# Row sums of squares of a differential-attention head: from one-column float32 products to ScalarE squares on transposed tiles

## The chip, the cores and the metric

One core of one Trainium2 chip runs the whole layer. The metric is the device time of one launch in microseconds (us); less is better. The engines are named as in the profile: PE is the matrix engine (PEld its weight loads), DVE the vector engine, ACT the scalar engine (activations), POOL the general engine, SP the queue that issues most transfers. Each engine works through its own instructions in the order in which the program gives them, and an instruction that needs another engine's result waits at the head of its queue.

## The reference, cut to what matters

The layer has a token mixer (differential attention with four heads and sparse attention with eight heads that read the same input) and a feed-forward part. The change touches the end of a differential head only:

```python
def rms_norm(x, g):
    xf = x.astype(jnp.float32)
    y = xf * lax.rsqrt(jnp.mean(xf * xf, axis=-1, keepdims=True) + NORM_EPS)
    return (y * g.astype(jnp.float32)).astype(x.dtype)
...
    o_diff = diff_attention(dq, dk, dv, lam)
    o_diff = (rms_norm(o_diff, diff_subln) * (1.0 - lam_init)).reshape(B, S, DIFF_WIDTH)
```

For each of the 512 tokens and each of the four heads, the head's output has 128 values. The mean of their squares is needed, its inverse root scales the 128 values, and each of the 128 positions also has a gain of its own, `diff_subln * (1 - lam_init)`.

## The kernel before, in words

The kernel is written for a sequence of 512 tokens, four blocks of 128. In the attention part a differential head is called `D0` to `D3`, a sparse head `N0` to `N7`. The order of all work is written out by hand in a string called `PLAN`: each word is a step, and the steps are issued from first to last. So the place of a step in `PLAN` decides its place in the queue of every engine that it uses, relative to all other steps on that engine.

A step's name is the head, then the operation. The digits behind a colon choose the buffers that the step takes. For steps in which PE opens a new result tile, that digit is one of the eight PSUM banks: `N1S02:6` opens bank 6. A bank may be opened again only when everyone who reads its former content is done.

The operations that matter here:

- `S..` scores on PE, `Q..` the causal mask added on PE, `X..` the row maximum on DVE, `E..` the exponential on ACT with its row sum (an ACTIVATE, and behind it an instruction that reads the accumulator). `X` and `E` read the bank of `S`. `D1S00:6` puts the scores of two token blocks into bank 6, and `D1E01` and `D1E00` read them.
- `T..` PE transposes the probabilities into a bank; `H..` ACT copies them out rounded (line 983), `L..` DVE takes the rest (line 986); `V..` products with the values on PE (line 1034 for `D`, 1156 for `N`).
- `SC`, `CX`, `PH`, `TC`, `HC` belong to the compressed branch of a sparse head, `KS1` and `KF1` to the compressed values (lines 870, 883, 886). `M0` to `M3` are early products of the output projection (line 1227), which are long runs on PE alone.

A differential head's output stands transposed: the 128 value positions on the partitions, the 512 tokens along the row, in one bank called `av`. The end of the head is, in steps: `SQ` (ACT squares the bank into an SBUF tile, line 1039), `O3` (ACT copies the bank into an SBUF tile times the gain per partition, line 1043), `MS` (PE multiplies each 128x128 block of squares with a column of ones, so that the sums over the partitions come out with tokens on the partitions, four columns; line 1048), `N1` (DVE adds the epsilon; line 1052), `N2` and `N3` (ACT, logarithm and exponential), `N4` (POOL, one Newton step), `RB` (PE spreads the four columns back over the partitions by transposes, line 1064), `ML` (DVE multiplies, line 1082), `OH` and `OL` (the result split into two parts).

Around the four `MS` steps the plan before runs, cut to what stands next to them:

```
... D1E01:3 N2SC:0 D1X00:7 v1d0 N0H02:11 N0L02 N0M10 D1R D0MS:3 N0H00 N0L00 N2CX:11 KF1 D1E00:1 D1Q01 N0T10:7 N1S02:6 D0N1 N0H10:00 ...
... N5S1:0 ... N5Q01 D1MS:2 N5Q1 N5X12:0 N3H10:00 N3L10 N5E00:0 N5E12:3 N5X01:2 N4g1 N3T11:6 ...
```

Of the kernel before, what the change touches and what calls it, by code (L numbers as in the profile page):

```python
# [27 lines left out]
DIFF_HEADS = 4  # L28
# [84 lines left out]
N7S0:3 D3S11:7 N5H00 G1:1 N4O2:0 N5TC:4 D3Q11 N7Q0 N5L00 D3X12:0 N6S11:5 N5HC:1 N7X10:6 N6S02:6 N5V00:2 D3E12:3 D3R
# [171 lines left out]
def hybrid_block_kernel(  # L285
# [6 lines left out]
    act, dve, pool, pe = nc.scalar, nc.vector, nc.gpsimd, nc.tensor  # L292
# [6 lines left out]
    turn = [None]  # L299
# [702 lines left out]
    def diff_head(h, qd, kd, dv):  # L1002
        pp, hs = [{}, {}], {}
# [24 lines left out]
        def avs(u):  # L1028
            for j in JS[u]:
                if j == 0:  # L1030
                    hs["av"] = ps("av")
                for n, (vi, t) in enumerate(((0, 0), (1, 0), (0, 1))):
                    v0 = vi * 256 + (h % 2) * P
                    pe.matmul(hs["av"][:, j * P:], dv[j][:, v0:v0 + P], blocks(hs["pt"][t], j),  # L1034
                              start=(j == 0 and n == 0), stop=(j == NT - 1 and n == 2))

        def square():
            hs["sq"] = tslot("sq", tag="o")
            act.activation(hs["sq"], hs["av"], AF.Square)

        def weigh():
            hs["o32"] = tslot("o32", tag="o")
            act.activation(hs["o32"], hs["av"], AF.Copy, scale=gsub)

        def sums():
            hs["ms"] = ps("ms")
            for i in range(NT):
                pe.matmul(hs["ms"][:, i:i + 1], hs["sq"][:, i * P:(i + 1) * P], ones, start=True, stop=True)
# [17 lines left out]
        def out_high():  # L1066
# [9 lines left out]
        ops.update(  # L1076
            SQ=square, O3=weigh, MS=sums,
            N1=norm_in,
            N2=lambda: act.activation(hs["r"][1], hs["r"][0], AF.Ln),
            N3=lambda: act.activation(hs["r"][1], hs["r"][1], AF.Exp, scale=-0.5),  # L1080
            N4=newton, RB=spread,
            ML=lambda: dve.tensor_tensor(hs["sq"], hs["o32"], hs["rb"], OP.mult),
            OH=out_high,
# [243 lines left out]
    rr, pre, sq, rt, rv = ([None] * NT for _ in range(5))  # L1327
# [724 lines left out]
```

## Time and profile before

| what | value |
|---|---|
| time, median of 3 runs | 613.69 us (613.07 to 614.32) |
| the profiled execution's own time | 614.05 us |
| its span in the profile | 612.2 us |
| PE busy | 603.4 us, 99% of the span |
| DVE busy | 545.4 us, 89% |
| ACT busy | 373.7 us, 61% |
| POOL busy | 101.9 us, 17% |
| granted PE clock | 0.996 |

How to read it: the span is what the profile covers, and 614.05 minus 612.2, about 1.9 us, lies around it. The busy time of PE includes matrix products whose ends are modelled from a pipeline, so that a duration is longer than the distance to the next start; for the price of an instruction in a stream the distance between starts is the better number. ACT shows the same overlap: an ACTIVATE's duration is about 0.1 us longer than the distance to the next one. The timeline prints start and duration in us, engine, line, operation, output and inputs, and merges neighbours of one kind into one row with their count; a bracket at the end tells of idle time before it and who ended it. The windows view gives busy us of each engine in a stretch. The attention part with the four heads' ends runs from about 139 to 247 us of the span.

### The profile page before, as it was taken

Reading aid. Unit: us, or ns where it says so; the run is one execution under the profiler, and the core shown is the slowest. Engines: PE = TensorE matmul, PEld = TensorE weight load, DVE = VectorE, ACT = ScalarE, POOL = GpSimd, SP = SyncE. Lnnn points to the kernel's source line nnn. Section 1 sums busy time; section 2 is a strip of 40 time slices with the busy share of each in tenths; the row PEclk is TensorE's granted clock in tenths of the full one; section 3 lists DMA queues with packets and bytes.
Section 4 is the critical chain, followed back from the end, with each engine's and each line's share of the span. In section 5 each row is a group of like instructions: output and inputs, shape, how many; then the busy total and the mean of one; then the engine's idle time right before and its main releaser. Section 6 shows DMA issues by size and latency. Waiting matters only on the chain.

```text
span 612.2 us, 11013 instructions
## 1 busy us (share of the span) xinstructions
PE 603.4 (99%) x4066; PEld 548.5 (90%) x4066; DVE 545.4 (89%) x967; ACT 373.7 (61%) x784; POOL 101.9 (17%) x154
## 2 busy tenths in 40 slices
PE   9999999999999999999999999999999999999995
PEld 6888888899999989889999999999999988888884
DVE  5898888998899884899999998899999899999977
ACT  6445375467998886568585555555553666577522
POOL 0030000307868789100000000000000000000001
PEclk9999999999999999999999999999999999999998
DMA  8667786755342301654143444344342554576413
GB/s 260 204 221 276 243 308 229 247 210 187 105 122 90 101 35 39 203 201 177 38 171 105 138 138 138 105 139 172 124 138 84 173 172 164 186 247 229 137 40 133
DMA packets 38487, 98.42 MB, mean 161 GB/s; under 512 B 4257, under 2 KB 12065, under 8 KB 37537
## 3 DMA queue, kind: packets, MB, share of 16 engines
q1 hardware_dynamic: 38000, 97.45, 47.2%
q8 instruction: 32, 0.52, 0.4%
q10 hardware_dynamic: 432, 0.27, 0.1%
q14 instruction: 23, 0.18, 0.1%
HBM read 82.10 MB, written 15.60 MB: 160 GB/s over the span
## 4 chain that ended last, share of the span: by engine, by line
PE 91%; DVE 6%; DMA 1%; ACT 1%; issue 1%; DVEq 0%
PE yz L1494 26%; PE acc L1568 14%; PE fm L609 9%; PE fm L590 6%; PE mix L1241 5%; PE x L1494 4%; PE tr L973 4%; PE v L725 4%; PE avn L1156 3%; PE g L725 2%; PE sc L942 2%; PE sc L943 2%; PE mixp L1227 2%; PE cmp L824 1%; PE av L1034 1%; PE acc L1717 1%
## 5 line engine op out<-in xcount | busy, mean ns | idle before, releaser
L1774 POOL TENSOR_TENSOR uf<-c,gain 128x512 f32<-128x512 f32 x1 | 1.3, 1283 | 353.4 <-DVE c L1739 353.4
L956 ACT ACTIVATE p<-sc,nm 128x256 f32<-128x256 f32 (+3 forms) x96 | 50.5, 531 | 13.0 <-DVE nm L952 12.4
L952 DVE TENSOR_REDUCE nm<-sc 128x1 f32<-128x384 f32 (+3 forms) x96 | 43.0, 482 | 5.5 <-PE sc L948 3.4
L1494 PE MATMUL yz<-rope,wbh 128*128 128x256 f32 x352 | 47.2, 276 | 0.0
L1125 POOL TENSOR_TENSOR p<-p,l 128x256 f32<-128x256 f32 (+3 forms) x64 | 45.3, 732 | 0.9
L1494 PEld LDWEIGHTS yz<-rope,wbh 128*128 128x128 f32 x352 | 43.3, 188 | 0.0
L986 DVE TENSOR_TENSOR ptl<-tr,pth 128x384 fp32r<-128x384 f32 (+1 forms) x60 | 34.3, 591 | 8.8 <-ACT pth L983 8.8
L983 ACT ACTIVATE pth<-tr 128x384 fp32r<-128x384 f32 (+1 forms) x60 | 30.2, 528 | 6.9 <-PE tr L973 6.7
L1471 ACT ACTIVATE weh<-e 128x1024 fp32r<-128x1024 f32 x22 | 23.3, 1058 | 16.0 <-DVE e L1453 12.5
L1479 DVE TENSOR_TENSOR wel<-e,weh 128x1024 fp32r<-128x1024 f32 x22 | 26.8, 1220 | 3.4 <-ACT weh L1471 2.9
L1471 ACT ACTIVATE wbh<-wraw 128x1024 fp32r<-128x1024 f32 x22 | 23.3, 1059 | 10.3 <-DVE wraw L1458 6.4
L973 PE MATMUL tr<-ident,p 128*128 128x128 f32 x200 | 27.7, 273 | 0.0
L1479 DVE TENSOR_TENSOR wbl<-wraw,wbh 128x1024 fp32r<-128x1024 f32 x22 | 26.9, 1221 | 0.9 <-ACT wbh L1471 0.9
L1471 ACT ACTIVATE whi<-wraw 128x1024 fp32r<-128x1024 f32 x22 | 23.1, 1055 | 7.3 <-DMA wraw<-in_wg 7.1
L1617 ACT ACTIVATE whi<-wraw 128x1024 fp32r<-128x1024 f32 x20 | 21.0, 1056 | 10.7 <-PE acc L1568 6.5
L1494 PE MATMUL yz<-rope,wbl 128*128 128x256 f32 x176 | 27.2, 276 | 0.0
L1479 DVE TENSOR_TENSOR wlo<-wraw,whi 128x1024 fp32r<-128x1024 f32 x22 | 26.8, 1219 | 0.0
L1623 DVE TENSOR_TENSOR wlo<-wraw,whi 128x1024 fp32r<-128x1024 f32 x20 | 24.2, 1222 | 2.0 <-ACT whi L1617 2.0
L1494 PEld LDWEIGHTS yz<-rope,wbl 128*128 128x128 f32 x176 | 23.3, 188 | 0.0
L1524 ACT ACTIVATE us<-yz 128x512 f32<-128x512 f32 x22 | 13.0, 592 | 16.9 <-PE yz L1494 16.7
L973 PEld LDWEIGHTS tr<-ident,p 128*128 128x128 f32 x200 | 22.4, 141 | 0.7
L942 PE MATMUL sc<-kst,qst 128*128 128x384 f32 (+3 forms) x64 | 22.9, 366 | 0.0
(385 smaller groups left out, 1996.6 us busy)
## 6 DMA issues: line engine op xcount, KB each, us to landing
wraw<-in_wg SPq DMA_DIRECT2D x24, 512.0 KB, 3.7
wraw<-in_wu SPq DMA_DIRECT2D x22, 512.0 KB, 3.3
wraw<-in_wd SPq DMA_DIRECT2D x22, 512.0 KB, 3.7
qk<-rope SPq DMA_DIRECT2D x7, 1024.0 KB, 5.2
kst<-qk SPq DMA_DIRECT2D x24, 256.0 KB, 4.4
wraw<-in_wf SPq DMA_DIRECT2D x10, 512.0 KB, 4.7
wraw<-in_wo SPq DMA_DIRECT2D x8, 512.0 KB, 4.3
qst<-qk SPq DMA_DIRECT2D x16, 256.0 KB, 2.7
```

The source lines that it names most:

```text
L590: pe.matmul(st["fm", m][:, s], blk[k][w][:, m * P:(m + 1) * P], xx[k][:, s], start=first, stop=True, skip_group_check=True)
L609: pe.matmul(st["fm", m], fms[m][w][:, k * P:(k + 1) * P], xx[k], start=(c == 0 and k == 0), stop=(c == 2 and k == NK - 1))
L725: pe.matmul(pts[i], xx[k][:, i * P:(i + 1) * P], ws[c][wi][:, off:off + n], start=(m == 0), stop=(m == 3 * NK - 1))
L942: pe.matmul(sv[i], lhs, kk[:, 0, :w], start=(n == 0), stop=False, skip_group_check=True)
L952: dve.tensor_reduce(nm[i], sv[i], AX.X, OP.max, negate=True)
L956: act.activation(pp[i], sv[i], AF.Exp, bias=nm[i], accum_out=hs["l"][:, row, i:i + 1])
L973: pe.transpose(tr[:, n * P:(n + 1) * P], pp[i][:, j * P:(j + 1) * P], ident)
L1125: pool.tensor_tensor(p, p, hs["l"][:, 1 + br, i:i + 1].to_broadcast(list(p.shape)), OP.mult)
L1471: act.activation(t[0], w[src], AF.Copy)
L1479: dve.tensor_tensor(t[1], W[f][PARTS[n][0]], f32(t[0]), OP.subtract)
L1494: pe.matmul(o, W[f][w][wi][:, k * P:(k + 1) * P], hop[h][hi][:, k * HS:(k + 1) * HS], start=(n < 3 and m == 0), stop=(m == 11), skip_group ...
L1568: pe.matmul(acc[t], a[x][:, t * P:(t + 1) * P], b[y], start=(first and n == 0), stop=(last and n == 2))
```

## The change

The sums of squares no longer come from PE. `SQ` and `MS` change places in kind and in order. First `O3` copies the bank `av` plainly into SBUF (no gain any more). Then `MS` transposes the four 128x128 blocks of this copy on PE into a bank `ot`, so that tokens are on the partitions. Then `SQ`, four ACT instructions, squares the four blocks out of that bank and sums along the row in the accumulator, one column of four each. `N1` takes these four columns from SBUF, not from PSUM. The gain moves into `ML`, which becomes a DVE instruction with two multiplications.

In the plan `O3` stands where `SQ` stood, and `SQ` stands directly behind `MS` (for `D3` and `D2`, too). The later place of `O3` is gone for `D1`, `D2` and `D3`. `D2RB` moves a few steps later, and some `O1` steps take another buffer. The diff, with the plan cut to the places that differ (`-` before, `+` after):

```diff
-D1S00:6 D1S10:4 D0V1 D0V2 N0PH:0 D1Q02 D1X03:0 gd2 D0SQ:2 N0M02 D1Q11 LW1:0 N0M00 D1Q10 D0O3:1 D1E03:3 N0M11 D1X12:6
+D1S00:6 D1S10:4 D0V1 D0V2 N0PH:0 D1Q02 D1X03:0 gd2 D0O3:1 N0M02 D1Q11 LW1:0 N0M00 D1Q10 D1E03:3 N0M11 D1X12:6
...
-D1E11:0 KS1:1 D1S01:4 v1a0:n LW6:1 D1E01:3 N2SC:0 D1X00:7 v1d0 N0H02:11 N0L02 N0M10 D1R D0MS:3 N0H00 N0L00 N2CX:11 KF1
+D1E11:0 KS1:1 D1S01:4 v1a0:n LW6:1 D1E01:3 N2SC:0 D1X00:7 v1d0 N0H02:11 N0L02 N0M10 D1R D0MS:3 D0SQ:2 N0H00 N0L00 N2CX:11 KF1
...
-D0ML N2E11:3 N1T02:6 N1TC:4 N2E13:3 N1H01:00 N0O2:0 N3SC:2 N2g0 D1SQ:1 N1H02 N1T11:1 D2LD1:0 N1L01 N1T12:3 N3CX:02 N2M01
-N2R1 N2M02 N1HC:1 N1H12:11 N1H11 N1L02 N3S01:5 N3S02:2 D1O3:0 D2S02:4 N1L12 N3S1:6 N1T00:3 N3Q02 N3Q01 N1H00 N1L11
+D0ML N2E11:3 N1T02:6 N1TC:4 N2E13:3 N1H01:00 N0O2:0 N3SC:2 N2g0 D1O3:0 N1H02 N1T11:1 D2LD1:0 N1L01 N1T12:3 N3CX:02 N2M01
+N2R1 N2M02 N1HC:1 N1H12:11 N1H11 N1L02 N3S01:5 N3S02:2 D2S02:4 N1L12 N3S1:6 N1T00:3 N3Q02 N3Q01 N1H00 N1L11
...
-N3T10:3 N4M00 N5Q11 N6LD:2 N5S01:4 N5S1:0 D2LE D2H2 D2L1 D2L2 N5E10:1 N5Q01 D1MS:2 N5Q1 N5X12:0 N3H10:00 N3L10 N5E00:0
+N3T10:3 N4M00 N5Q11 N6LD:2 N5S01:4 N5S1:0 D2LE D2H2 D2L1 D2L2 N5E10:1 N5Q01 D1MS:2 D1SQ:1 N5Q1 N5X12:0 N3H10:00 N3L10 N5E00:0
...
-D3LD1:0 D2SQ:2 N4T11:5 N4HC:1 D3Q01 D2MS:6 N4H11:11 N4L00 N5M12 D3S10:2 D2O3:0 N4H01 N5M11 D3Q10 D3X02:0 N4T12:3 D2N1
+D3LD1:0 D2O3:2 N4T11:5 N4HC:1 D3Q01 D2MS:6 D2SQ:0 N4H11:11 N4L00 N5M12 D3S10:2 N4H01 N5M11 D3Q10 D3X02:0 N4T12:3 D2N1
...
-N5T10:2 N4V10 N6CE N5H11:00 D2N4 N6X00:7 N5PL N6CS D2RB:7 N5H10 N5T12:4 N4V11 N5L11 D3E03:0 N4V12 D1OH:35 D3S12:3 N5M02
+N5T10:2 N4V10 N6CE N5H11:00 D2N4 N6X00:7 N5PL N6CS N5H10 N5T12:4 N4V11 N5L11 D3E03:0 N4V12 D2RB:7 D1OH:35 D3S12:3 N5M02
...
-N7E11:0 N6M10 N6M13 N7CS N7S12:6 D3V2 N7E10:3 N7R0 N6PL N7Q12 N7g0 N6L00 D3SQ:0 N6T10:2 N6H02 N6T01:7 N6H01 N7X13:7
-N6L02 N7E13:0 N6L01 N7M00 N6H10:11 N7S11:0 W6c:1 D3MS:3 N7CM N7M02 N7Q11 N7M01 N6L10 N7X12:5 N7PH:1 N6T11:5 N6TC:1
+N7E11:0 N6M10 N6M13 N7CS N7S12:6 D3V2 N7E10:3 N7R0 N6PL N7Q12 N7g0 N6L00 D3O3:2 N6T10:2 N6H02 N6T01:7 N6H01 N7X13:7
+N6L02 N7E13:0 N6L01 N7M00 N6H10:11 N7S11:0 W6c:1 D3MS:3 D3SQ:1 N7CM N7M02 N7Q11 N7M01 N6L10 N7X12:5 N7PH:1 N6T11:5 N6TC:1
...
-D3N2 N7M10 N5OL M2:2 N6V12 D3N3 D3O3:1 N7T12:5 N7T11:1 N7H12:11 D3N4 N7T10:3 W2d:k N7L12 D3RB:4 N7V00:0 N7H10 N7L10
+D3N2 N7M10 N5OL M2:2 N6V12 D3N3 N7T12:5 N7T11:1 N7H12:11 D3N4 N7T10:3 W2d:k N7L12 D3RB:4 N7V00:0 N7H10 N7L10
...
+        def take():
+            hs["o32"] = tslot("o32", tag="o")
+            act.activation(hs["o32"], hs["av"], AF.Copy)
+
+        def turn():
+            hs["ot"] = ps("ot")
+            for i in range(NT):
+                c = slice(i * P, (i + 1) * P)
+                pe.transpose(hs["ot"][:, c], hs["o32"][:, c], ident)
+
         def square():
             hs["sq"] = tslot("sq", tag="o")
-            act.activation(hs["sq"], hs["av"], AF.Square)
-
-        def weigh():
-            hs["o32"] = tslot("o32", tag="o")
-            act.activation(hs["o32"], hs["av"], AF.Copy, scale=gsub)
-
-        def sums():
-            hs["ms"] = ps("ms")
+            hs["r"] = [U.tile([P, NT], F32, tag=f"dr{j}", name="dr", bufs=DIFF_HEADS) for j in range(4)]
             for i in range(NT):
-                pe.matmul(hs["ms"][:, i:i + 1], hs["sq"][:, i * P:(i + 1) * P], ones, start=True, stop=True)
+                c = slice(i * P, (i + 1) * P)
+                act.activation(hs["sq"][:, c], hs["ot"][:, c], AF.Square, accum_out=hs["r"][1][:, i:i + 1])
 
         def norm_in():
-            hs["r"] = [U.tile([P, NT], F32, tag=f"dr{j}", name="dr", bufs=DIFF_HEADS) for j in range(4)]
-            dve.scalar_tensor_tensor(hs["r"][0], hs["ms"][:, :NT], 1.0 / P, hs["le"], OP.mult, OP.add)
+            dve.scalar_tensor_tensor(hs["r"][0], hs["r"][1], 1.0 / P, hs["le"], OP.mult, OP.add)
...
-            SQ=square, O3=weigh, MS=sums,
+            SQ=square, O3=take, MS=turn,
...
-            ML=lambda: dve.tensor_tensor(hs["sq"], hs["o32"], hs["rb"], OP.mult),
+            ML=lambda: dve.scalar_tensor_tensor(hs["sq"], hs["o32"], gsub, hs["rb"], OP.mult, OP.mult),
```

More of the change, by code (lines that the diff above doesn't have):

```diff
@@ L106 @@
 D2V0:0 N4H00 D2V1 N4L02 N5CE N6CX:11 D2V2 D1RB:6 LW2:2 N5CS D3E01:0 N5R1 N4TC:7 N5g1 D3S01:4 N5R0 D3E00:3 W1l D1ML
-D3LD1:0 D2SQ:2 N4T11:5 N4HC:1 D3Q01 D2MS:6 N4H11:11 N4L00 N5M12 D3S10:2 D2O3:0 N4H01 N5M11 D3Q10 D3X02:0 N4T12:3 D2N1
+D3LD1:0 D2O3:2 N4T11:5 N4HC:1 D3Q01 D2MS:6 D2SQ:0 N4H11:11 N4L00 N5M12 D3S10:2 N4H01 N5M11 D3Q10 D3X02:0 N4T12:3 D2N1
 N4T10:7 N4L11 LW7:0 N6S01:6 N4L01 D3S02:0 N4H12 N4V00:5 D3X11:1 N4VC D3X10:2 N6S0:1 N4V01 N4L12 N4V02 N4H10 D3E10:2 D2N2
 N6Q01 D3Q02 D2N3 N5M13 D3E11:2 N5g0 N7LD:1 N5M10 N5CM N4L10 N5PH:0 N6Q0 D3E02:2 N5T11:3 N6CA W2a:0 D3X03:6 N6X02:3
-N5T10:2 N4V10 N6CE N5H11:00 D2N4 N6X00:7 N5PL N6CS D2RB:7 N5H10 N5T12:4 N4V11 N5L11 D3E03:0 N4V12 D1OH:35 D3S12:3 N5M02
+N5T10:2 N4V10 N6CE N5H11:00 D2N4 N6X00:7 N5PL N6CS N5H10 N5T12:4 N4V11 N5L11 D3E03:0 N4V12 D2RB:7 D1OH:35 D3S12:3 N5M02
 N5M01 N6S1:0 N5M03 N5L10 N5M00 N5H12 N3OH:7i D1OL N6E02:0 D2ML N7SC:2 N3OL D3Q12 W7b:m N5L12 N6Q1 N5T01:7 N7CX:02 W7a:f
-D3X13:5 N5H01:11 N6X11:4 N6X01:2 N5L01 N6E00:1 N5T00:6 N5T02:4 N5H02 W7c:b M1:2 N5L02 D3E13:1 N6X10:1 W7d:8 N4O1:0
+D3X13:5 N5H01:11 N6X11:4 N6X01:2 N5L01 N6E00:1 N5T00:6 N5T02:4 N5H02 W7c:b M1:2 N5L02 D3E13:1 N6X10:1 W7d:8 N4O1:2
 N7S0:3 D3S11:7 N5H00 G1:1 N4O2:0 N5TC:4 D3Q11 N7Q0 N5L00 D3X12:0 N6S11:5 N5HC:1 N7X10:6 N6S02:6 N5V00:2 D3E12:3 D3R
@@ L117 @@
 N6R1 G0 D3T1:2 D3T2:7 D3H1 N7X00:3 D3L0 N6T00:1 N6g1 D3H2 D3V0:4 N6H00:00 N6PH:0 D3L1 D3L2 N6M12 D3V1 N6M11 N7E00:2
-N7E11:0 N6M10 N6M13 N7CS N7S12:6 D3V2 N7E10:3 N7R0 N6PL N7Q12 N7g0 N6L00 D3SQ:0 N6T10:2 N6H02 N6T01:7 N6H01 N7X13:7
-N6L02 N7E13:0 N6L01 N7M00 N6H10:11 N7S11:0 W6c:1 D3MS:3 N7CM N7M02 N7Q11 N7M01 N6L10 N7X12:5 N7PH:1 N6T11:5 N6TC:1
+N7E11:0 N6M10 N6M13 N7CS N7S12:6 D3V2 N7E10:3 N7R0 N6PL N7Q12 N7g0 N6L00 D3O3:2 N6T10:2 N6H02 N6T01:7 N6H01 N7X13:7
+N6L02 N7E13:0 N6L01 N7M00 N6H10:11 N7S11:0 W6c:1 D3MS:3 D3SQ:1 N7CM N7M02 N7Q11 N7M01 N6L10 N7X12:5 N7PH:1 N6T11:5 N6TC:1
 N6HC:0 N6V00:6 N7M03 N5OH:l9 N6V01 W2b:a N7E12:2 M3:7 D2OH:en N7R1 N6VC N7PL N6H11 N6V02 N6L11 D3N1 N7TC:2 N7g1 N7T01:1
 N6T12:0 N7HC:0 N7M13 N7T00:5 N7M12 D2OL N7T02:3 N7H01:00 N7H00 N7H02 N7M11 N7L00 N6V10 N7L01 N6V11 N6H12 N7L02 N6L12
-D3N2 N7M10 N5OL M2:2 N6V12 D3N3 D3O3:1 N7T12:5 N7T11:1 N7H12:11 D3N4 N7T10:3 W2d:k N7L12 D3RB:4 N7V00:0 N7H10 N7L10
-N7V01 W6d:6 N7H11 N6O1:2 N7L11 N7V02 N7V10 N7VC D3ML N7V11 D3OH:g2 D3OL N7V12 N6O2:0 N7O1:1 N7O2 N7OH:cj G2 G3 N7OL
+D3N2 N7M10 N5OL M2:2 N6V12 D3N3 N7T12:5 N7T11:1 N7H12:11 D3N4 N7T10:3 W2d:k N7L12 D3RB:4 N7V00:0 N7H10 N7L10
+N7V01 W6d:6 N7H11 N6O1:0 N7L11 N7V02 N7V10 N7VC D3ML N7V11 D3OH:g2 D3OL N7V12 N6O2:0 N7O1:2 N7O2 N7OH:cj G2 G3 N7OL
 """
```

## The prediction

> **What bounds the kernel now.** I read the page first, then busy time by stretches of 14 us over the attention part, then the timeline of PE and ACT around each of the four sums. The first line to see is the page's busy line; the next rows are the stretches in which the sums of heads 0, 1 and 2 lie. Columns: stretch, its length, then busy us and instructions of PE, PEld, DVE, ACT, POOL, then the granted clock, the transfers' share and GB/s.
>
> ```profile
> PE 603.4 (99%) x4066; PEld 548.5 (90%) x4066; DVE 545.4 (89%) x967; ACT 373.7 (61%) x784; POOL 101.9 (17%) x154
> ...
> 136.00:150.00 14.00, 14.00 (x115) 13.43 (x114) 10.74 (x27) 9.26 (x32) 10.43 (x15) 1.00 0.67 226
> 192.00:206.00 14.00, 14.00 (x114) 13.16 (x112) 12.93 (x33) 13.07 (x43) 9.92 (x18) 1.00 0.34 114
> ```
>
> PE never stands in these stretches and is 99% busy over the span, so work taken off it is worth its full time, and a wait put into it costs its full time: behind the attention PE has nothing to catch up with. The page's 61% for ACT is an average over the span; between 192 and 206 us ACT is busy 13.07 of 14 us and DVE 12.93. What ACT does later there, PE may have to wait for.
>
> **What PE gains.** The sums are eight PE passes of one column for the four products; each loads 128 weights.
>
> ```profile
> 145.30 1.00 PE L1048 MATMUL ms<-ones,sq 128*128 128x1 f32 x8
> 146.17 0.22 PE L948 MATMUL sc<-mask_b,ident_b 128*128 128x128 bf16 x1
> 146.22 0.60 PE L973 MATMUL tr<-ident,p 128*128 128x128 f32 x4
> 146.58 0.48 PE L942 MATMUL sc<-kst,qst 128*128 128x512 f32 x1
> 146.90 0.39 PE L943 MATMUL sc<-kst,qst 128*128 128x512 f32 x1
> 147.12 0.63 PE L916 MATMUL sc<-kst,qst 128*128 128x512 f32 x2
> ```
>
> From the start of the sums to the next start is 146.17 - 145.30 = 0.87 us. Four float32 transposes, which the new `MS` is, take 146.58 - 146.22 = 0.36 us, and the score behind them steps on after 0.32 us where the next one takes 0.22, so up to 0.1 more hangs on them. In heads 1 and 2 the sums take 0.86 us each (rows below, 194.71 - 193.85 and 204.21 - 203.35). So PE saves 0.4 to 0.5 us a head; I take 0.42, and 4 x 0.42 = 1.7 us in all. That is the change's direct worth if nobody waits.
>
> **What ACT pays.** Before: one square of 512 columns and one copy with a gain. After: a plain copy, then four squares of 128 columns, each with an accumulator read. Prices, from starts:
>
> ```profile
> 139.96 0.60 ACT L1039 ACTIVATE sq<-av 128x512 f32<-128x512 f32 x1 [0.56 <-PE av L1034]
> 140.46 0.69 ACT L1043 ACTIVATE o<-av,gsub 128x512 f32<-128x512 f32 x1
> 141.03 0.69 ACT L956 ACTIVATE p<-sc,nm 128x512 f32<-128x512 f32 x1
> ...
> 272.85 0.60 ACT L1355 ACTIVATE pre<-mix 128x512 f32<-128x512 f32 x1 [1.37 <-PE mix L1241]
> 273.35 0.19 ACT L1355 ACTIVATION_READ_ACCUMULATOR pre<-mix 128x1 f32 x1
> ...
> 158.47 0.38 ACT L956 ACTIVATE p<-sc,nm 128x128 f32<-128x128 f32 x1
> 158.72 0.22 ACT L956 ACTIVATION_READ_ACCUMULATOR p<-sc,nm 128x1 f32 x1
> ...
> 605.48 0.42 ACT L1754 ACTIVATE uj<-c 128x256 bf16<-128x256 f32 x1 [0.40 <-DVE c L1739]
> 605.80 0.18 ACT L1754 ACTIVATION_READ_ACCUMULATOR uj<-c 128x1 f32 x1
> 605.89 0.40 ACT L1754 ACTIVATE uj<-c 128x256 bf16<-128x256 f32 x1
> ```
>
> The square costs 0.50 us to the next start, the copy with a gain 0.57; a plain copy I put at the square's 0.50. A square of 128 columns with an accumulator is not in this trace. Squares of 512 and 256 columns durations differ between 0.60 and 0.40, so 128 columns last about 0.30, 0.30 below the 512 ones, and step on after 0.50 - 0.30 = 0.20 at most; the exponential of 128 columns, which carries a bias, steps on after 0.25. The accumulator read steps on after 0.09. So a square with its read is 0.25 to 0.34 us. I take 0.27, nearest to the squares, since the new ones carry no bias: 4 x 0.27 = 1.08 us. Each head then costs ACT 1.08 + 0.50 - 0.50 - 0.57 = 0.5 us more. As a sum, 2 us in 110, that is little. Its place is what matters.
>
> The Trainium skill, page "ScalarE: Activation LUTs", section "What ACT_TABLE_LOAD costs", gives 186 ns + 0.833 ns per column with immediate operands, some 93 ns more for a pointer operand and an overlap of 93 ns. As an estimate by that page a square of 128 columns steps on after 186 + 107 - 93 = 200 ns, 0.29 with the read, and the sum below would be 0.2 us higher; the trace's 0.57 against 0.50 with and without a gain agrees with the pointer's price.
>
> **Where ACT has to wait, head 0.** In the new plan `D0SQ` stands directly behind `D0MS`, ahead of `N0H00`, `KF1` and `D1E00` on ACT. ACT is far ahead of PE there:
>
> ```profile
> 144.04 0.98 ACT L983 ACTIVATE pth<-tr 128x384 fp32r<-128x384 f32 x2
> 144.89 0.30 ACT L883 ACTIVATE vcs<-kvc 128x128 fp32r<-128x128 f32 x1
> 145.04 0.40 ACT L956 ACTIVATE p<-sc,nm 128x128 f32<-128x128 f32 x1
> 145.29 0.25 ACT L956 ACTIVATION_READ_ACCUMULATOR p<-sc,nm 128x1 f32 x1
> 146.92 0.60 ACT L983 ACTIVATE pth<-tr 128x512 fp32r<-128x512 f32 x1 [1.38 <-PE tr L973]
> ```
>
> The second of the two in the first row is `N0H00`; it ends at 144.04 + 0.98 = 145.02 and lasts 0.60 like the 512-column copy at 146.92, so it begins at 144.42. `D1E00` is the row at 145.04. The transposes start on PE at 145.30 at the earliest and last 0.60 (the row of four above), to 145.90. From the end of those transposes (146.22 + 0.60 = 146.82) to ACT's read at 146.92 is 0.10, so the first square starts at 146.00: ACT stands 1.6 us from 144.42 on. The four squares end their turn at 147.08. From `N0H00` to `D1E00` the trace has 145.04 - 144.42 = 0.62, so `D1E00` runs from 147.70 to 148.10. It is the last reader of bank 6 (`D1S00:6`), and the next to open bank 6 is `N1S02:6`, the PE row at 146.58. PE would be there at 146.16 and stands until 148.15: a wait of 2.0 us, net 148.15 - 146.58 = +1.6 us. The idle time of ACT of 1.38 us comes later and doesn't help `D1E00`. Behind PE's wait ACT is in step again. DVE is held too: `N0L00` waits for `N0H00`, whose end moves from 145.02 to 147.08 + 0.60 = 147.7, and the maxima and `L` steps queue behind it, banks of PE with them; PE's own 1.6 us cover most of these 2.7, and for the banks that DVE frees last I add 0.1.
>
> **Head 1.** `D1SQ` stands ahead of `N3H10` and `N5E00`.
>
> ```profile
> 193.49 0.63 ACT L983 ACTIVATE pth<-tr 128x512 fp32r<-128x512 f32 x1
> 193.96 0.41 ACT L956 ACTIVATE p<-sc,nm 128x128 f32<-128x128 f32 x1
> ...
> 193.85 1.00 PE L1048 MATMUL ms<-ones,sq 128*128 128x1 f32 x8
> 194.71 0.27 PE L922 MATMUL sc<-mask_b,ident_b 128*128 128x256 bf16 x1
> 194.82 0.82 PE L973 MATMUL tr<-ident,p 128*128 128x128 f32 x6
> ```
>
> The transposes end at 193.85 + 0.60 = 194.45, the squares run from 194.55 to 195.63, `N3H10` takes 193.96 - 193.49 = 0.47, and `N5E00` ends at 195.63 + 0.47 + 0.41 = 196.51 instead of 194.37. It frees bank 6 for `N3T11:6`, PE's row at 194.82: net 196.55 - 194.82 = +1.7 us.
>
> **Heads 2 and 3.**
>
> ```profile
> 203.00 0.63 ACT L1148 ACTIVATE pct<-trc 128x512 fp32r<-128x512 f32 x1
> 203.49 0.52 ACT L983 ACTIVATE pth<-tr 128x384 fp32r<-128x384 f32 x1
> ...
> 203.35 1.00 PE L1048 MATMUL ms<-ones,sq 128*128 128x1 f32 x8
> 204.21 0.31 PE L942 MATMUL sc<-kst,qst 128*128 128x128 f32 x1
> 205.56 0.42 PE L942 MATMUL sc<-kst,qst 128*128 128x384 f32 x1
> ...
> 231.59 0.95 PE L1048 MATMUL ms<-ones,sq 128*128 128x1 f32 x8
> ...
> 232.49 0.62 ACT L983 ACTIVATE pth<-tr 128x512 fp32r<-128x512 f32 x1
> 237.99 0.60 ACT L1148 ACTIVATE pct<-trc 128x512 fp32r<-128x512 f32 x1 [1.84 <-PE trc L1144]
> ```
>
> In head 2 the squares run from 203.35 + 0.60 + 0.10 = 204.05 to 205.13 and are themselves the last readers of bank 6, which `N6S01:6` opens at 205.56, or at 205.14 with PE's gain: the last square's end lies within 0.1 us of that. Net -0.3. The copy at 203.49 starts 1.6 us later, less the 0.57 of `O3` that goes, and DVE's share of that may give back 0.2: -0.1. In head 3 ACT is behind PE (the square's place is after the copy at 232.49), the transposes are long done, the delay of some 0.6 to 1 us ends in ACT's idle 1.84 us, and PE's early products of the projection need none of it: -0.4 for PE, and I give back 0.2 for a transpose whose bank DVE reads later: -0.2.
>
> **Other parts.** `ML` with two multiplications on DVE: nothing, since the multiplication with a scalar and a tensor from PSUM lasts what the plain one lasts, 683 against 676 ns, 0.03 us in all.
>
> ```profile
> L625 DVE SCALAR_TENSOR_TENSOR rope<-fm,sin 128x512 f32<-128x512 f32 x14 | 9.6, 683 | 1.6 <-PE fm L609 1.5
> L1082 DVE TENSOR_TENSOR sq<-o,rsb x4: 648/676/679, 161.5 to 246.2; 128x512 f32<-128x512 f32 x4
> ```
>
> `N1` now waits for ACT; DVE reaches it in head 0 after the delayed `N0L00`, later than the squares end, so it queues nothing up. `D2RB` moves behind four products on PE and the row of `ML` follows it: nothing is near. `av` comes free 0.5 us earlier, and no PE row waits for it. No transfer is moved, neither on SP's nor on POOL's queue.
>
> **The sum.** +1.6 + 0.1 + 1.7 - 0.1 - 0.2 = +3.1; the direct gain is in each. I take +3.0 against the profiled 614.05 us, 617.0; that execution is 0.36 us over the median of 613.69, so the median after would be 616.7.
>
> The lower bound: the first square needs only the first block of the transposes. Then it starts three steps of 0.36 / 4 earlier, 0.27 us in heads 0, 1 and 2, 0.8 less: +2.2; with squares of 0.25 +2.0. No row decides it, as each reader in the trace takes the whole bank; the nearest, the copy at 146.92, starts after the fourth transpose, and I take that. The upper bound: squares at 0.34 add 0.28 in heads 0 to 2, +0.8: +3.8.
>
> By the Trainium skill, page "PSUM — Partial Sum Buffer", section "PSUM bank collisions raise a hardware error", two engines must not touch one bank at once, so the first square would come after the last transpose, as in my sum and not in its lower bound; no run here shows it.
>
> **The rivals.** First, a gain: ACT's delay stays within the slack. It decides at the PE row at 146.58: `D1E00` left the bank at 145.44, so PE, 0.42 early, has 0.7 us of room, against the 2.7 us by which `D1E00` moves. It needs bank 6 free without ACT's queue holding it, with squares that run behind `D1E00`; the rows of ACT here follow the plan's order, which speaks against it. Then 1.7 us come off: 612.0. Second, the squares start block by block as above: 615.9. Third, the squares cost what the exponentials cost: 617.5. Fourth, two standstills of 2 us make PE's clock drop as at the start of the program, where 512 columns step on after 3.17 / 7 = 0.45 us and not the 0.22 of above:
>
> ```profile
> 1.02 3.17 PE warm L420 x7
> ```
>
> Another 3.2 us at half rate cost 1.6 each, 3.2 in all: 619.9. The clock is 1.00 in the rows of stretches and PE never pauses in them, so the trace before can't tell. The Trainium skill, page "TensorE: Matmul & The Clock Gate", section "What's actually happening", puts that drop at an idle window of about 3.4 us; a wait of 2.0 is shorter, and by that rule the clock holds.
>
> **Chances.** My sum 0.45, block by block 0.2, dear squares 0.17, the clock 0.04, a gain 0.08, and 0.06 that the delays cancel to nothing: ACT's later idle time taken up by a plan that has more room than I see. About 0.2% (1.2 us) is what a measurement of this kernel tells from no change. Faster 0.08; within 0.2%, the 0.06 and another 0.06 of the low end of block by block, 0.12; slower the rest, 0.80. The range takes in the bounds 615.7 and 617.5 and about 1 us on either side, as much as the smaller terms of heads 2 and 3 and of DVE's banks could be off together: 614.8 to 618.6. Slower cases alone hold most of the chance.
>
> **What would show it.** In the profile after: four transposes of 0.36 to 0.45 us where the sums were; idle time of ACT before the first square ended by PE, about 1.6 us in head 0 and 1.0 in head 1; idle time of PE ended by ACT's exponential, near 2 us, before the score behind `D0MS` and before the transposes behind `D1MS`, and next to none in heads 2 and 3; PE's last row of the attention some 3 us later. If PE shows no idle time at these two places, the prediction is wrong at its main step.

## The result, and the profile after

The changed kernel takes 619.25 us (median of 6 runs, 617.63 to 622.12) against 614.18 us of the kernel before beside it: 1.0094 times as long, 95% interval 1.0075 to 1.0114. In two later sets it took 619.08 and 619.40 us, ratios 1.0081 [1.0061, 1.0100] and 1.0085 [1.0068, 1.0102]. It is slower, as forecast, but by 5.1 us and not by 3.0, and 619.25 lies above the range. The profiled execution shown here took 621.63 us, its span is 619.8 us.

The page's busy line, then the two stretches of 14 us in which the sums of heads 0 and 1 lie (stretch, length, busy us and instructions of PE, PEld, DVE, ACT, POOL, granted clock, transfers' share, GB/s):

```profile
PE 605.6 (98%) x4050; PEld 547.6 (88%) x4050; DVE 546.8 (88%) x967; ACT 375.9 (61%) x812; POOL 101.9 (16%) x154
```

```profile
136.00:150.00 14.00, 12.26 (x96) 11.49 (x94) 8.68 (x22) 8.88 (x34) 10.19 (x14) 1.00 0.70 226
192.00:206.00 14.00, 12.04 (x81) 10.56 (x79) 10.01 (x24) 11.71 (x45) 9.12 (x18) 0.88 0.38 120
```

PE was busy for all 14.00 us of both stretches; now it stands for 1.74 and 1.96 us in them, and in the second the mean of its granted clock is 0.88. The view of PE's waits (what waited, for whom, us, times, longest) names ACT's exponential in both:

```profile
PE tr L973 <- ACT p L956: 2.0, 1, 2.0
PE sc L942 <- ACT p L956: 1.7, 1, 1.7
```

The timeline of ACT and PE at head 0, and at head 1 (start, duration, and in brackets the idle time ahead with what ended it):

```profile
144.56 0.49 ACT L983 ACTIVATE pth<-tr 128x384 fp32r<-128x384 f32 x1
146.46 0.28 ACT L1052 ACTIVATE sq<-ot 128x128 f32<-128x128 f32 x1 [1.41 <-PE ot L1045]
...
147.48 0.61 ACT L983 ACTIVATE pth<-tr 128x512 fp32r<-128x512 f32 x1
...
148.12 0.41 ACT L956 ACTIVATE p<-sc,nm 128x128 f32<-128x128 f32 x1
...
145.82 0.61 PE L1045 MATMUL ot<-ident,o 128*128 128x128 f32 x4
146.26 0.22 PE L948 MATMUL sc<-mask_b,ident_b 128*128 128x128 bf16 x1
...
148.67 0.50 PE L942 MATMUL sc<-kst,qst 128*128 128x512 f32 x1 [1.74 <-ACT p L956]
...
197.07 0.28 ACT L1052 ACTIVATE sq<-ot 128x128 f32<-128x128 f32 x1 [0.86 <-PE ot L1045]
...
198.56 0.40 ACT L956 ACTIVATE p<-sc,nm 128x128 f32<-128x128 f32 x1
...
199.10 1.20 PE L973 MATMUL tr<-ident,p 128*128 128x128 f32 x6 [1.96 <-ACT p L956]
199.96 0.77 PE L942 MATMUL sc<-kst,qst 128*128 128x512 f32 x1
...
237.71 0.60 PE L1045 MATMUL ot<-ident,o 128*128 128x128 f32 x4
```

Read it from the top: ACT has copied at 144.56 and then stands 1.41 us, since the next thing in its queue, the first square, needs PE's transposes of 145.82. Squares and reads take 146.46 to 147.48, four turns of 0.255 us, then come two copies, and only at 148.12 the exponential that frees bank 6. PE has been ready for that bank since the end of the transposes ahead of it, 1.74 us before, and starts at 148.67. The gain is there too: from the transposes to the next start it is 146.26 - 145.82 = 0.44 us, where the sums took 0.87.

To compare executions that began a little earlier or later, I take the distance from the start of `D0MS` to the start of `D3MS` on PE. Before it is 231.59 - 145.30 = 86.29 us (both rows stand in the prediction). Here it is 237.71 - 145.82 = 91.89: 5.6 us more. The prediction's terms for this stretch sum to +1.6 + 0.1 + 1.7 - 0.1 = +3.3.

### The profile page after: what moved, and what is told of

Same layout as the page of the kernel before. It is cut to its first block, busy times and chain, and to the rows that moved or that the text cites. A ratio compares the mean times of both kernels' runs of the same rounds, so it can differ in the third digit from the quotient of the medians.

```text
span 619.8 us, 11007 instructions
## 1 busy us (share of the span) xinstructions
PE 605.6 (98%) x4050; PEld 547.6 (88%) x4050; DVE 546.8 (88%) x967; ACT 375.9 (61%) x812; POOL 101.9 (16%) x154
## 4 chain that ended last, share of the span: by engine, by line
PE 87%; DVE 7%; DMA 3%; ACT 2%; issue 1%; DVEq 0%; ACTq 0%
PE yz L1497 25%; PE acc L1571 13%; PE fm L609 8%; PE fm L590 5%; PE mix L1244 5%; PE x L1497 4%; PE tr L973 3%; PE avn L1159 3%; PE v L725 3%; PE g L725 2%; PE sc L942 2%; PE mixp L1230 2%; PE sc L943 2%; PE av L1034 1%; DMA wraw<-in_kw 1%
```

## The experiments

The main theory: ACT, standing for the transposes in front of its own queue, holds bank 6, and PE stands for it. The rival: ACT's added work costs the time, wherever it stands. Open was also why the clock fell behind the wait of head 1, and whether it always does.

**The changed kernel again** (no edit).

> The changed kernel once more, as the yardstick of this set. Main theory (ACT, standing for the transposes in front of its queue, holds bank 6, and PE stands for it in heads 0 and 1; in head 1 the clock drops behind that): about 619.3 us, PE waits of about 2.0 us at the score behind `D0MS` and of 1.7 to 2.0 at the transposes behind `D1MS`, granted clock 0.6 to 0.8 between 198 and 204 us. If the slow clock of head 1 was an accident of one execution, the clock is 1.00 there this time and the time is nearer to 617.6.

619.08 us. In its profiled execution, which took 618.92 us:

```profile
144.74 0.61 PE L1045 MATMUL ot<-ident,o 128*128 128x128 f32 x4
...
198.03 0.99 PE L973 MATMUL tr<-ident,p 128*128 128x128 f32 x6 [1.96 <-ACT p L956]
198.78 0.48 PE L942 MATMUL sc<-kst,qst 128*128 128x512 f32 x1
...
235.18 0.60 PE L1045 MATMUL ot<-ident,o 128*128 128x128 f32 x4
```

```profile
192.00:206.00 14.00, 12.04 (x92) 10.84 (x91) 11.20 (x29) 12.77 (x49) 8.21 (x17) 1.00 0.43 142
```

The same wait of 1.96 us, and the clock stays at 1.00: the score behind it lasts 0.48 us where it lasted 0.77. The distance is 90.44 us, +4.15, so the drop is worth 91.89 - 90.44 = 1.45 us where it comes, and it does not always come. This execution still took 618.92 us, not the 617.6 that was expected without the drop: it lost 1.4 us around 426 us, in the feed-forward part.

**The squares behind the exponentials.** The plan alone is edited:

```diff
-... D0MS:3 D0SQ:2 N0H00 N0L00 N2CX:11 KF1 D1E00:1 D1Q01 ...
+... D0MS:3 N0H00 N0L00 N2CX:11 KF1 D1E00:1 D0SQ:2 D1Q01 ...
-... D1MS:2 D1SQ:1 N5Q1 N5X12:0 N3H10:00 N3L10 N5E00:0 N5E12:3 ...
+... D1MS:2 N5Q1 N5X12:0 N3H10:00 N3L10 N5E00:0 D1SQ:1 N5E12:3 ...
```

> `D0SQ` and `D1SQ` moved behind the exponentials `D1E00` and `N5E00` on ACT; the work of every engine stays what it is in the changed kernel. Main theory: ACT has read bank 6 before it stands for the transposes, both waits of PE vanish, the clock stays at 1.00, and only PE's direct gain of about 0.42 a head is left, less what later ACT work gives back: 613.2 to 613.9 against 614.2. Rival (ACT's added work costs the time, wherever it stands): 618 to 619.

615.65 us, 1.0028 [1.0017, 1.0039]. Neither theory had it: 3.4 us came off, both waits of 2 us are gone and the clock is 1.00, but the kernel is still slower than before.

```profile
145.37 0.61 PE L1045 MATMUL ot<-ident,o 128*128 128x128 f32 x4
...
146.12 2.40 POOL L1269 TENSOR_TENSOR wlo<-wraw,whi 128x1024 fp32r<-128x1024 f32 x1
...
147.37 1.16 DVE L1055 SCALAR_TENSOR_TENSOR dr<-dr,le 128x4 f32<-128x4 f32 x1
...
153.24 0.54 PE L1147 MATMUL trc<-ident_r,pcs 128*128 128x128 f32 x4 [0.43 <-ACT p L956]
...
197.09 0.51 PE L942 MATMUL sc<-kst,qst 128*128 128x512 f32 x1 [0.61 <-ACT p L956]
...
233.64 0.60 PE L1045 MATMUL ot<-ident,o 128*128 128x128 f32 x4
```

New, smaller waits: 0.43 and 0.20 us behind head 0, 0.61 in head 1, where the squares now hold up `N5E12`, the last reader of the next score's bank. The distance is 88.27, +1.98. One row is odd: `N1`, four columns, lasts 1.16 us on DVE and ends at 148.53, as GpSimd's subtraction ends at 148.52.

**The wait of head 1 filled with products.**

```diff
+    mask1 = ops["N5Q1"]
+    ops["N5Q1"] = lambda: [mask1() for _ in range(18)]
```

> The changed kernel, with the causal mask of `N5Q1` added 18 times in place of once (17 more products of 256 bf16 columns at 0.11 us, 1.8 us): PE multiplies through most of the wait of head 1 in place of standing. Output values hardly change, the mask is only larger. If PE's standstill there drops the clock: the wait shrinks to about 0.2 us, the clock between 198 and 204 us stays near 1.00, and 1.6 us come off against the changed kernel, 617.6. If the clock drops for another reason: the slow rows stay and the time is 619.3. The work of the wait itself costs nothing by either.

618.31 us, 0.8 below the changed kernel beside it (1.0081 [1.0062, 1.0100] against the kernel before), half of what was expected.

```profile
196.21 2.13 PE L922 MATMUL sc<-mask_b,ident_b 128*128 128x256 bf16 x18
```

PE multiplies through the wait, the score is no earlier, and the clock there is 1.00. The mean granted clock of the six runs is 0.9972, like that of the kernel before (0.9970 over 21 runs), where the changed kernel beside it has 0.9960.

**Squares that wait for nothing.**

```diff
-                act.activation(hs["sq"][:, c], hs["ot"][:, c], AF.Square, ...)
+                act.activation(hs["sq"][:, c], hs["o32"][:, c], AF.Square, ...)
```

> The squares at their places read the outputs before they are turned (sums along the wrong axis, so the values are not the layer's) and so wait for nothing; ACT's work is the same, the transposes stay on PE. Main theory: in head 0 `D1E00` ends about 1.1 us later than in the kernel before and PE waits 0.35, net 0; in head 1 `N5E00` ends 1.1 later, PE waits about 1.1, net +0.7, and the clock holds; heads 2 and 3 give 0.3 back: 614.6 us. Rival (the added work costs all of it): 619.3.

615.15 us, 1.0019 [1.0008, 1.0030]. The waits of PE, and the timeline:

```profile
PE tr L973 <- ACT p L956: 1.1, 1, 1.1
...
PE sc L942 <- ACT p L956: 0.3, 1, 0.3
```

```profile
145.60 0.61 PE L1045 MATMUL ot<-ident,o 128*128 128x128 f32 x4
...
144.71 0.32 ACT L1052 ACTIVATE sq<-o 128x128 f32<-128x128 f32 x1
...
233.54 0.60 PE L1045 MATMUL ot<-ident,o 128*128 128x128 f32 x4
```

Both waits have the forecast sizes; the time is 0.5 us above the 614.6 expected. With all of the work at the same places and ACT no longer standing, the distance is 87.94, +1.65 against +4.15: the standing makes 2.5 us, and the rest stays with ACT's work in front of the exponentials and what hangs on it. The main theory holds for the larger part, the rival for the smaller.

**The clock by itself.** A kernel of its own; its core, with `gap` a product, n copies on ACT of its bank, and a product into that bank:

```diff
+    for n in (2, 3, 4, 5, 6, 8):
+        for r in range(4):
+            gap(n); busy(62 + 5 * r)
+    for n in (2, 3, 4, 5):
+        for r in range(4):
+            flanked(n, 5, 6); busy(62 + 5 * r)
+    for n in (20, 40, 60):
+        for r in range(4):
+            turns(n); busy(62 + 5 * r)
```

> Nothing of the layer is computed here: TensorE runs stretches of 62 to 77 ordinary products of 512 columns (14 to 17 us), and between two of them stands (a) a gap made by 2, 3, 4, 5, 6 or 8 copies on ACT that it waits for, about 1.1, 1.6, 2.1, 2.6, 3.1 and 4.1 us, (b) gaps of 2 to 5 copies with 5 float32 transposes ahead and 6 behind, as in head 1, or (c) 20, 40 or 60 transposes without a gap, about 1.8, 3.6 and 5.4 us; each four times. If only standing counts and the limit is near 3.4 us, as the Trainium skill (page "TensorE: Matmul & The Clock Gate", section "What's actually happening") has it, the clock drops behind the gaps of 4.1 us alone. My theory (transposes do not count as work for the clock): it drops also behind the flanked gaps of about 2 us and more, in some of the four, and behind 3.6 and 5.4 us of transposes, and does not behind plain gaps of 1.1 to 2.1 us. If a plain gap of 2 us is enough, it drops behind those too.

First the timeline at two gaps of three copies and at one stretch of 60 transposes, then busy time and clock by stretches (granted clock third from the end): two in which the first gap lies and the 3.4 us behind it, the one in which the second gap lies and the one behind it, and the 3.4 us at the end of the transposes:

```profile
98.96 0.50 PE L80 MATMUL b<-a,w 128*128 128x512 f32 x1 [2.01 <-ACT dump L89]
...
152.80 0.79 PE L80 MATMUL b<-a,w 128*128 128x512 f32 x1 [2.01 <-ACT dump L89]
...
1003.08 6.71 PE L85 MATMUL tr<-ident,raw 128*128 128x128 f32 x60
```

```profile
94.75:98.17 3.42, 2.21 (x10) 1.50 (x8) 0.00 (x0) 1.08 (x2) 0.00 (x0) 1.00 0.00 0
98.17:101.58 3.41, 2.62 (x11) 2.18 (x12) 0.00 (x0) 0.71 (x2) 0.00 (x0) 1.00 0.00 0
99.10:102.50 3.40, 3.40 (x15) 2.79 (x16) 0.00 (x0) 0.00 (x0) 0.00 (x0) 1.00 0.00 0
149.37:152.78 3.41, 1.43 (x7) 0.85 (x5) 0.00 (x0) 1.79 (x3) 0.00 (x0) 1.00 0.00 0
152.78:156.19 3.41, 3.39 (x8) 2.71 (x9) 0.00 (x0) 0.00 (x0) 0.00 (x0) 0.50 0.00 0
1009.60:1013.00 3.40, 3.40 (x17) 2.81 (x16) 0.00 (x0) 0.00 (x0) 0.00 (x0) 1.00 0.00 0
```

Two gaps of 2.01 us, to the hundredth the same: behind one 15 products start in 3.4 us, behind the other 8. Counting gaps behind which the steps between products doubled:

| idle time of PE, us | 1.4 | 2.0 | 2.6 | 3.3 | 3.9 | 5.2 |
|---|---|---|---|---|---|---|
| plain gap | 0 of 4 | 1 of 4 | 3 of 4 | 3 of 4 | 4 of 4 | 4 of 4 |
| gap between transposes | 0 of 4 | 2 of 4 | 2 of 4 | 4 of 4 | | |

Where the steps doubled, a gap cost 1.35 to 2.8 us in the steps behind it. Behind 20, 40 and 60 transposes without a gap (2.4 to 6.7 us) the steps doubled in none of 12. So my theory on transposes falls: they keep the clock. A plain standstill of 2 us is enough, not always, and one of 1.4 us never was.

The granted clock in this trace tells what decides. Its stretches of half clock begin whole multiples of 3.413 us apart (at 152.78, 176.67 and 193.74, 7 and 5 steps) and last one or two such steps, so the trace can be cut into windows on that grid, as the rows above are. A border between two windows cuts the first gap into 1.21 and 0.79 us of idle time (3.42 - 2.21 and 3.41 - 2.62). The second gap lies in one window, with 1.98 us (3.41 - 1.43), and the window behind it runs at half clock. The same rule sorts all 40 gaps: where the clock held, no window had more than 1.87 us of idle time (17 gaps), and where it fell, one had 1.96 us or more (23 gaps).

It also fits head 1. The first row is the window with its wait in the changed kernel's first profile, where the clock fell at 199.74; the other two are the two windows over which the same wait is split in the profile of the second:

```profile
196.33:199.74 3.41, 1.45 (x12) 1.01 (x12) 1.64 (x4) 2.67 (x15) 3.39 (x5) 1.00 0.10 41
...
193.11:196.52 3.41, 2.97 (x24) 2.41 (x22) 2.42 (x7) 2.53 (x13) 2.93 (x6) 1.00 0.69 245
196.52:199.93 3.41, 1.90 (x14) 1.64 (x15) 1.96 (x5) 3.27 (x16) 2.44 (x5) 1.00 0.00 1
```

All 1.96 us in one window there, 0.44 and 1.51 here. Head 0's wait of 1.74 us is too short for the rule in any place. The grid lies otherwise in each execution (the clock records of the two traces begin on it at 5.17 and at 5.37 us), so an execution with the drop and one without can be the same program.

The Trainium skill, page "TensorE: Matmul & The Clock Gate", puts the limit at an idle window of about 3.4 us in its section "What's actually happening", and holds in "Part 4: PE-mode transpose" that transposes do not count as busy in the same way; this record agrees with neither, with drops from 1.96 us of idle time in a window on and none behind 6.7 us of transposes.

**`N1` of head 0 on GpSimd.** As the kernel with the squares behind, and

```diff
-            dve.scalar_tensor_tensor(hs["r"][0], hs["r"][1], 1.0 / P, hs["le"], OP.mult, OP.add)
+            if h == 0:
+                pool.tensor_scalar(hs["r"][0], hs["r"][1], 1.0 / P, 0.0, OP.mult, OP.add)
+                pool.tensor_tensor(hs["r"][0], hs["r"][0], hs["le"], OP.add)
+            else: ...
-... N1S02:6 D0N1 N0H10:00 ... W4l N0H01 N1Q02 ...
+... N1S02:6 N0H10:00 ... W4l N0H01 D0N1 N1Q02 ...
```

> As the kernel with `D0SQ` and `D1SQ` behind the exponentials (615.65 us), but `N1` of head 0 runs on GpSimd, behind its `W4l`, in place of VectorE. Theory (in head 0 `N1`, now with two operands in SBUF, lasts 1.16 us in place of 0.16 since GpSimd's subtraction of 2.4 us runs beside it, and PE later waits 0.43 and 0.20 us for exponentials whose maxima came late): VectorE goes on 1 us earlier, both PE waits go, 0.6 to 0.9 us come off, 614.9. Rival (the squares on ACT make those waits, not `N1`): same as that kernel, 615.6.

614.35 us, 1.0008 [0.9998, 1.0018]: 1.3 us off, more than expected, and no longer to be told from the kernel before.

```profile
145.40 0.61 PE L1045 MATMUL ot<-ident,o 128*128 128x128 f32 x4
...
147.40 0.56 DVE L952 TENSOR_REDUCE nm<-sc 128x1 f32<-128x384 f32 x1
...
232.56 0.60 PE L1045 MATMUL ot<-ident,o 128*128 128x128 f32 x4
```

DVE comes to its maxima at 147.40, where `N1` stood until 148.53; both PE waits behind head 0 are gone, and the distance falls to 87.16, +0.87. The wait of head 1 is still there, with 0.59 us.

**`D1SQ` later still.** On top of that:

```diff
-... N5E00:0 D1SQ:1 N5E12:3 ... N3T11:6 D1N1 N3H11 N4M13 D1N2 D1N3 ... N3H12 N5S02:1 N5E11:3 ... N5CA D1N4 ...
+... N5E00:0 N5E12:3 ... N3T11:6 N3H11 N4M13 ... N3H12 N5S02:1 D1SQ:1 N5E11:3 ... D1N1 N5CA D1N2 D1N3 D1N4 ...
```

> As the kernel with `N1` of head 0 on GpSimd, and `D1SQ` moved on behind `N3H12`, with `D1N1` to `D1N3` behind that. Theory (in head 1 the squares stand ahead of `N5E12`, which holds the bank of the next score; ACT is 93% busy there and only has room of some 0.25 us later): PE's wait of 0.6 us ahead of the score goes, but a part of it comes back at later exponentials, 0.3 to 0.8 us off, 614.2 to 614.7 with the theory on `N1`. Rival (ACT is full, every place costs the same): no change against that kernel.

614.93 us, 1.0016 [1.0004, 1.0028], against 614.35 for the kernel with `N1` on GpSimd. Its profile has `D0MS` and `D3MS` here:

```profile
145.05 0.61 PE L1045 MATMUL ot<-ident,o 128*128 128x128 f32 x4
...
232.02 0.60 PE L1045 MATMUL ot<-ident,o 128*128 128x128 f32 x4
```

86.97, +0.68: 0.2 us gained inside the attention, which the times do not show. That is the rival's outcome: neither place tried behind the exponential in this stretch, where ACT was 13.07 of 14 us busy before, takes the squares for nothing.

**Sums with one pass, in the kernel before.** Squares written rounded, products with two columns of ones, and the other slots adjusted:

```diff
+    ones_r = cpool.tile([P, 2], F32R, name="ones_r")
-                pe.matmul(hs["ms"][:, i:i + 1], hs["sq"][:, i * P:(i + 1) * P], ones, start=True, stop=True)
+                pe.matmul(hs["ms"][:, 2 * i:2 * i + 2], hs["sr"][:, i * P:(i + 1) * P], ones_r, start=True, stop=True)
```

> The kernel before, with its sums as products of squares rounded to the one-pass float32 format (two columns of ones, one product a block) in place of two-pass float32 products; nothing is transposed and ACT's work stays as before. Theory (PE is the bound and only work taken off it without new ACT work or order counts): four passes in place of eight, 0.87 to about 0.44 us a head, 1.7 us in all, 612.3. Rival (PE's direct gain is eaten elsewhere, as it is in the change): 613.5 to 614.

620.52 us, 1.0113 [1.0096, 1.0131]: a miss by 8 us. Up to 300 us PE was 0.4 us ahead of the kernel before; then it fell back steadily, by 6.5 us until 487 us. Nothing of the sums is there. But the new constant moved every tile behind it by 32 bytes.

**The same at the old addresses, and the shift alone.** For the first, the constant takes half of the pad ahead; for the second the kernel before only gets a larger pad:

```diff
-    cpool.tile([P, 16], F32, name="cpad")
+    cpool.tile([P, 8], F32, name="cpad")
+    ones_r = cpool.tile([P, 2], F32R, name="ones_r")
```

```diff
-    cpool.tile([P, 16], F32, name="cpad")
+    cpool.tile([P, 24], F32, name="cpad")
```

> The kernel with one-pass sums of rounded squares again (620.52 us, of which the stretch of the feed-forward products alone, from 300 to 490 us, lost 7 us), but the two columns of ones take their 32 bytes from a pad ahead of them, so that every other tile lies at the address it has in the kernel before. Theory (the 32 bytes moved all tiles to another alignment, and the products that read them step on slower; the sums themselves gain): the drift between 300 and 490 us is gone, and PE's gain of 0.3 to 0.43 a head is left: 612.3 to 613.0. Rival (the drift comes from the sums or the order of the slots): 620.5 again.

> The kernel before with 32 bytes more of padding ahead of its constants and nothing else: all tiles behind it move by 32 bytes. Theory (the alignment cost the 7 to 8 us of the kernel with one-pass sums): 620.5 to 622.5. Rival (that kernel lost them by its sums): 614.

613.17 us, 0.9987 [0.9976, 0.9998], for the sums at the old addresses, and 620.36 us, 1.0111 [1.0098, 1.0124], for the shift. One stretch of the feed-forward products, before and with the shift alone:

```profile
320.00:480.00 160.00, 160.00 (x1414) 160.00 (x1414) 152.52 (x221) 87.67 (x142) 0.00 (x0) 1.00 0.39 129
```

```profile
320.00:480.00 160.00, 160.00 (x1364) 160.00 (x1363) 147.39 (x213) 81.51 (x131) 0.00 (x0) 1.00 0.37 125
```

1364 products in place of 1414 in the same 160 us, at the same clock, with PE busy throughout: 117.3 ns each in place of 113.2. The 32 bytes cost 6.75 us, nearly all that the kernel with the moved tiles had lost. With the addresses kept, the one-pass sums show

```profile
145.22 0.58 PE L1051 MATMUL ms<-ones_r,sq 128*128 128x2 f32 x4
145.67 0.23 PE L950 MATMUL sc<-mask_b,ident_b 128*128 128x128 bf16 x1
...
193.40 0.58 PE L1051 MATMUL ms<-ones_r,sq 128*128 128x2 f32 x4
...
194.10 1.13 PE L975 MATMUL tr<-ident,p 128*128 128x128 f32 x6
...
231.01 0.50 PE L1051 MATMUL ms<-ones_r,sq 128*128 128x2 f32 x4
```

0.45 us a head in place of 0.87, no transposes, no work for ACT, distance 85.79, -0.50. It is the one version that beats both kernels, by 0.4 us, 0.13% [0.02%, 0.24%], where 0.6 to 1.3 were expected, hardly more than can be told from no change. Three heads at 0.42 us would have shortened the distance by 1.3. Head 1 gives nothing of it: from the start of its sums to the end of the transposes behind them it takes 194.10 + 1.13 - 193.40 = 1.83 us, against 194.82 + 0.82 - 193.85 = 1.79 before, because the six transposes now last 1.13 us. What they wait for was not followed, nor the rest.

**Both waits filled, beside the changed kernel.** As with head 1 filled, and `D1Q01` 31 times.

```diff
+    mask0 = ops["D1Q01"]
+    ops["D1Q01"] = lambda: [mask0() for _ in range(31)]
```

> The changed kernel a third time, as the yardstick of this set: 619.2 us; mean granted clock of its runs about 0.995, against 0.997 of the kernel before.

> The changed kernel with both waits of PE filled: the mask of `D1Q01` added 31 times and that of `N5Q1` 18 times in place of once each (1.65 and 1.8 us of bf16 products of 128 and 256 columns; the masked scores only get a larger negative number). Theory (a standstill of about 2 us closes the clock in some executions, for some 3.4 us at half rate, and in the others not): the mean granted clock of the runs is 0.997 as in the kernel before, and 0.8 to 1.3 us come off the median against the changed kernel: about 618. If the clock plays no part in the median: 619.2.

619.40 us, 1.0085 [1.0068, 1.0102], and 618.78 us, 1.0079 [1.0067, 1.0091]. The stretch of head 1 in the one and in the other:

```profile
192.00:206.00 14.00, 12.04 (x82) 10.80 (x81) 10.09 (x24) 11.81 (x44) 9.21 (x18) 0.88 0.37 118
```

```profile
192.00:206.00 14.00, 13.89 (x107) 12.36 (x104) 11.20 (x28) 12.76 (x47) 8.88 (x18) 1.00 0.45 150
```

The drop again in the changed kernel, as in two of its three profiles, and none where PE multiplies. The two fills took 0.8 and 0.6 us off the median, in the expected direction and less than the 1.6 and 0.8 to 1.3 expected; the intervals overlap, so the times alone don't prove it. By the records, the clock's mean is 0.9952 over the 18 runs of the changed kernel, 0.9969 over the 11 filled ones and 0.9970 over 61 of the kernel before in the later sets: as an estimate, 0.0018 of 617 us is 1.1 us of lost clock in an average run.

## Why the direction was right and the size wrong

- **The mechanism** was right, place by place. PE's two waits stand where they were forecast, with 1.74 and 1.96 us, and the first square starts 0.03 us after the end of the fourth transpose, so not block by block.
- **Head 0**: net +1.6 forecast. PE was 145.82 - 145.30 = 0.52 us later than before at `D0MS`, and 148.67 - 146.58 = 2.09 later behind the wait: +1.57. Right.
- **Banks that DVE frees last**: +0.1 forecast, 0.4 measured, at the score of `N2S1`. Mis-sized: DVE stood 2.2 us for the late copy and the maxima behind it came late.
- **Head 1**: +1.7 forecast, 1.8 measured (1.45 us of clock left aside). Right.
- **Heads 2 and 3**: head 2 was put at -0.1. In the profile without the drop `D2MS` starts at 206.72, so from there to `D3MS` it is 235.18 - 206.72 = 28.46 us, against 231.59 - 203.35 = 28.24 before: +0.2. Another 0.2 of the 4.15 (less 1.57, 0.4, 1.8 and 0.2) came in small steps ahead of it that no term held. So ACT's later copies did not find all the room that the forecast gave them; which of them PE waited for is not shown. Head 3 was right with -0.2: PE's products with `pth` behind the last early product start at 246.17 and 242.78, so the +4.15 is +3.95 there (246.17 - 144.74 less 242.78 - 145.30).
- **Prices**: 0.27 us for a square with its read, measured 0.25; a head's gain on PE 0.42, measured 0.43. `ML` was taken as free and lasts 742 ns where it lasted 676: 0.06 us each.

Two steps failed. The first is the small terms, DVE's banks (+0.1) and head 2 (-0.1): the attention up to `D3MS` took 4.15 us more and not 3.3, +0.9. The second is the fourth rival. The clock after a standstill got a chance of 0.04 because a wait of 2.0 us is shorter than the window of the Trainium skill's page "TensorE: Matmul & The Clock Gate", section "What's actually happening", and the trace before, in which PE never pauses, could not contradict that. In this case's runs 1.96 us of standing in one window of 3.41 us are enough, and behind head 1 the clock fell in two of three profiles. Its price for one drop, 1.6 us, was about right (1.45); its two drops in every execution were not, since head 0's wait never dropped the clock.

As an estimate the parts make 3.0 + 0.9 + 1.1 = 5.0 us, against 5.1 measured. Either failure alone would have stayed in the range that ended at 618.6 (614.18 + 3.9 = 618.1, and 614.18 + 4.1 = 618.3); both together left it. That 619.25 lies near the 619.9 of the fourth rival is luck: it counted two drops in each execution and none of the small terms.

The expectation for the kernel with the squares behind failed likewise, and showed a cost of the change that its own order hides: with `ms` in PSUM, `N1` had one operand in SBUF, and in the kernel before it lasted 0.16 us at 147.30, inside GpSimd's subtraction of 146.04 to 148.44; now it has two, and in the kernel with the squares behind it lasts until such a subtraction ends. In the changed kernel's own order `N1` of heads 0 and 1 comes later and lasts 0.16 us. The Trainium skill, page "SBUF — State Buffer", section "SBUF: two separate sides", says that a VectorE instruction with two SBUF operands and a GpSimd one that reads SBUF exclude each other; the row of 1.16 us, ending 0.01 us after GpSimd's, agrees.

Still open: the filled kernels, whose distance is 90.5 us in both profiles, 4.2 above the kernel before, ran 4.4 and 5.2 us longer. Single profiles of the changed kernel lost 1.3 us at 489 us or 1.4 at 426 us, in the feed-forward part, others nothing there. The profile of the kernel with `D1SQ` later, which has neither wait, lost time around 426 us, too. No run separates that from the scatter, which spans 3 us in the kernel before. So the clock's share of 1.1 us rests on the means of the clock; the fills alone show 0.6 to 0.8 us, within their noise.

## What to carry to other kernels

On an engine with a fixed order, an instruction that must wait costs what stands behind it: move the consumer behind everything that frees a bank before asking what it costs by itself. Count a standstill of TensorE of 2 us and more with half a clock of 3.4 us behind it; between 2 and 3.9 us it came or not by where the standstill fell in windows of 3.41 us that lie otherwise in each execution. Where a full engine takes over work from another full one, look for a cheaper form on the old engine first, and keep every address when adding a constant.

## What the runs showed of the hardware beyond the forecast

- TensorE's clock fell to half behind idle times from 2.0 us (1 of 4 plain gaps) to always at 3.9 us, never at 1.4 us. Half clock began on a grid of 3.413 us, behind a window with 1.96 us or more of idle time (23 of 23) and never behind 1.87 us or less (17 of 17). Up to 6.7 us of float32 transposes alone kept it at 1.00.
- A tile shift of 32 bytes made the feed-forward products 117.3 ns in place of 113.2, 6.75 us in the whole kernel. Which operand it is, and at which addresses, was not tried.
- A VectorE instruction of four columns with two SBUF operands lasted 1.16 us in place of 0.16 beside a GpSimd subtraction of 2.40 us.
